# Feed-forward parts of 16, 16 and 12 feature tiles instead of 12, 16 and 16, and the spreading of 1/rms one step later

## The chip, the cores and the metric

The kernel runs on one core of a Trainium2 chip. The metric is the device time of one execution in microseconds (us); the time given for a kernel is the median of several executions. The profile shows the core's engines: TensorE (PE, with its weight loads as PEld), VectorE (DVE), ScalarE (ACT), GpSimd (POOL) and the DMA queue of SyncE (SP).

## What is computed

An encoder trunk of two residual layers on 256 tokens of width 2048, in float32. Layer 0 mixes tokens by grouped-query attention, layer 1 by a gated linear recurrence. Behind each mixer stands a feed-forward layer of 5632 features:

```python
def swiglu(h, w_gate, w_up, w_down):
    return (jax.nn.silu(h @ w_gate) * (h @ w_up)) @ w_down
...
        x = x + mix
        x = x + swiglu(rms_norm(x, norm_ffn[i]), ffn_w_gate[i], ffn_w_up[i], ffn_w_down[i])
```

## The kernel before

**Precision.** Every weight half (8 tiles of 128x128, 512 KB) is loaded into `raw`, rounded on ScalarE to `hi` (L142) and its remainder `lo` is made on VectorE (L144). Activations are split in the same way. A product of two operands is then three matmuls, hi·hi, hi·lo and lo·hi (`product`, L370 to L375).

**Tiling of the feed-forward layer.** The 5632 features are 44 tiles of 128, in three parts whose sizes are `PARTS` (L28). A part first makes its features, in units of four tiles (512 columns of gate and of up; 11 units in a layer, numbered through), then runs the part's rows of the down projection and adds them to the residual stream `x_tok`. The down projection handles its four columns of 512 in two pairs, c = 0 and c = 2 (`down`, L594).

**Two columns at a time, in seven products.** `project_pair` (L361) runs two columns, for units gate and up, over steps n of two row tiles each. A step that stands in `forms` is done in seven products rather than eight: `seven_forms` (L310) builds sums of weights on VectorE and ScalarE, and at the last such step of a pair `merge` (L415) combines the four extra sums. Which steps these are is set by `THREE` (1, 3, 5), for units listed in `FOURTH` also step `MORE` = 7, whose own operand form is built in the first such unit and kept, and with another order of the steps. For the down projection `down_seven` (L173) gives `THREE` for parts of 16 tiles (8 steps) and only its first two for parts of 12 (6 steps, `SHORT`). In `down_plan` (L166) the steps up to the last in seven products take both columns together; the others follow, first for the one column, then for the other, so that the first column is finished two halves before the second.

**The last part of layer 0.** There the second pair of columns is `alone`: it is done in plain products, first all steps of column 2, then all of column 3 (L189, L615). The reason is in the next stage: as each column is finished, `norm.add(c)` (L500) puts six pieces of work on the list `owed`: squares and transposes (`first`), four lots of copies (`copies`), and the scaled operands xg (`operands`). `settle` deals out one piece (two when more than six are owed) after each half; with the last column, all that is left is done at once. The recurrence's first projection, `project_two` (L441), uses the operands of columns 0 and 1 first, then those of column 2, and those of column 3 last.

**1/rms.** In that norm the factor 1/rms isn't in the operands. `spread` (L548) makes two diagonal matrices from it, and TensorE multiplies them by ones so that every partition has the row (L557); the result `nrb` scales the projections' outputs in `conv_branch` (L931). TensorE's program is in the order in which it is written; `later(NORM, stage)` places this product so many steps behind the call, where `step` is called once for each three matmuls of `sums`. `project_two` has 32 steps.

**Order on the engines.** TensorE's order is that of the program. The other engines' orders are made by a scheduler that simulates the program, within constraints: in the feed-forward layers the casts and remainders of the weights follow each other (`in_line`), copies stay behind the cast before them, and by `not_after` the remainder of the fourth half from there comes behind the adds that empty a finished column's accumulators (L609). `hi` and `lo` have five buffers each, `raw` six. Weight loads are issued by SyncE's queue, those prefetched for the sums of the steps in seven products by GpSimd's.

The lines that place the work:

```python
        return pair_plan(range(n), SHORT - 2 if n == SHORT else 1 + TWO[-1])
...
        return () if alone else THREE[:2] if n == SHORT else THREE
...
                alone = l == 0 and p == len(PARTS) - 1 and c > 0
...
                        settle(2 if len(owed) > 6 else 1)
...
            later(NORM, stage)
```

Of the kernel before, what the change touches and what calls it, by code (L numbers as in the profile page):

```python
# [24 lines left out]
GROUP = NQ // NKV  # L25
NBLK = 8
DFF = 5632
PARTS = [12, 16, 16]  # L28
THREE, TWO, SHORT = (1, 3, 5), (2, 5), 6
READY = 6  # L30
FOURTH, FOUR_STEPS, MORE = (3, 7), (1, 0, 3, 2, 5, 4, 7, 6), 7
FIRST_STEPS = (0, 1, 2, 4, 3, 6, 5, 7)
HALF = 8
WIDE = 512
# [6 lines left out]
GRID_W = 64  # L41

WARM = 10
NORM = 31
FIRST = 6
KEY_SCALE = 20
KEY_TURN = (62, 68)
# [24 lines left out]
def trunk(ctx, tc, w, out):  # L72
# [93 lines left out]
    def down_plan(n, alone):  # L166
        if alone:
            return pair_plan(range(n), 0)
        return pair_plan(range(n), SHORT - 2 if n == SHORT else 1 + TWO[-1])
# [6 lines left out]
    def ffn_order(l, base):  # L176
# [7 lines left out]

        for p, n in enumerate(PARTS):
            for _ in range(n // FOUR):
# [5 lines left out]
            for c in range(0, len(down), n):  # L192
                alone = l == 0 and p == len(PARTS) - 1 and c > 0
                for k, cols in down_plan(n // 2, alone):
# [54 lines left out]
    def later(delay, fn):  # L249
        waiting.append((clock[0] + delay, fn))  # L250
# [230 lines left out]
    class Norm:  # L481
# [66 lines left out]
        def spread(self):  # L548
# [11 lines left out]

            later(NORM, stage)

# [288 lines left out]
    def ffn(norm, nxt):  # L851
# [56 lines left out]
        line.update(act=None, dve=None)  # L908
        for p, n in enumerate(PARTS):
            hid, units, forms = [], [], {}  # L910
            for i in range(n // FOUR):
                unit(hid, units, forms, n, sum(PARTS[:p]) // FOUR + i)
            last = p == len(PARTS) - 1
            if last and nxt is not None:
# [237 lines left out]
```

## Time and profile before

| | |
|---|---|
| median of 3 executions | 1951.66 us (1951.56 to 1951.9) |
| the profiled execution | 1952.23 us |
| its span, first to last instruction | 1950.5 us |
| granted TensorE clock | 1.000 |
| read from HBM | 434.17 MB |

An engine's share on the page is its busy time over the span. In a row of a timeline stand start, length, engine, line, operation, the tile written, the tiles read, their shapes and how many instructions of the kind ran in a row; in brackets the idle time before it and what ended that. The last down projection of layer 0 runs from 860.65 to 945.65 us; the recurrent block begins there.

### The profile page before, as it was taken

The numbers are of one execution on the slowest core, as the hardware profiler recorded it, in microseconds if no ns is written. First come the engines' busy times: TensorE is split into PE (matmuls) and PEld (weight loads), VectorE is DVE, ScalarE is ACT, GpSimd is POOL, SyncE is SP. The second block draws the span as 40 slices with busy tenths as digits, with TensorE's granted clock in tenths as the row PEclk, the third lists the DMA queues.
The fourth block names the chain that finished last, engine by engine and source line by source line (L and its number), as shares of the span: only waits on it lengthen the run. The fifth ranks groups of instructions, "written<-read, shape, count | busy, mean of one in ns | idle before, by whom it ended". The sixth has DMA issues, their size and how long they took to land.

```text
span 1950.5 us, 27665 instructions
## 1 busy us (share of the span) xinstructions
PE 1944.6 (100%) x9623; PEld 1652.3 (85%) x9623; DVE 1751.0 (90%) x2362; ACT 1368.1 (70%) x2089; POOL 243.6 (12%) x345
## 2 busy tenths in 40 slices
PE   9999999999999999999999999999999999999999
PEld 7888888888888888888999998888888888888887
DVE  6777899999999999999878886999999999989997
ACT  6666777765777556777799886767756776567763
POOL 0011001011011110101034331011001010111010
PEclk9999999999999999999999999999999999999999
DMA  9544667778687787777555546577777777777784
GB/s 346 190 144 136 203 218 240 227 249 266 207 257 236 259 258 229 236 228 236 197 179 181 194 156 220 175 240 241 254 222 249 239 256 247 241 238 248 234 262 145
DMA packets 138091, 438.08 MB, mean 225 GB/s; under 512 B 15456, under 2 KB 16352, under 8 KB 137696
## 3 DMA queue, kind: packets, MB, share of 16 engines
q1 hardware_dynamic: 109296, 358.44, 53.3%
q0 software_dynamic: 28512, 77.87, 15.7%
q8 instruction: 75, 1.23, 0.2%
q14 instruction: 64, 0.52, 0.1%
q10 hardware_dynamic: 144, 0.02, 0.0%
HBM read 434.17 MB, written 2.10 MB: 224 GB/s over the span
## 4 chain that ended last, share of the span: by engine, by line
PE 98%; ACT 1%; DVE 0%; DMA 0%; issue 0%; SPq 0%; DVEq 0%; ACTq 0%
PE acc L372 61%; PE pm L372 14%; PE acc L274 10%; PE acc L425 3%; PE acc L426 3%; PE acc L427 3%; PE pm L274 1%; PE pm L427 1%; PE pm L426 1%; PE pm L425 1%; PE pm L763 1%; PE pm L795 1%; PE pm L781 0%; DMA raw<-in_w_qkv_dram 0%; ACT sg L627 0%; PE pm L707 0%
## 5 line engine op out<-in xcount | busy, mean ns | idle before, releaser
L144 DVE TENSOR_TENSOR lo<-raw,hi 128x1024 fp32r<-128x1024 f32 (+1 forms) x607 | 725.6, 1222 | 82.3 <-ACT hi L142 81.6
L142 ACT CAST hi<-raw 128x1024 fp32r<-128x1024 f32 (+1 forms) x607 | 618.2, 1045 | 213.8 <-PE acc L372 127.8
L372 PE MATMUL acc<-hi,xg 128*128 128x512 f32 x1836 | 588.3, 389 | 0.0
L372 PEld LDWEIGHTS acc<-hi,xg 128*128 128x128 f32 x1836 | 344.6, 188 | 71.8
L372 PE MATMUL acc<-hi,act 128*128 128x512 f32 x1258 | 401.9, 390 | 0.5 <-DVE gl L950 0.5
L372 PE MATMUL acc<-lo,xg 128*128 128x512 f32 x918 | 357.1, 389 | 0.0
L372 PEld LDWEIGHTS acc<-hi,act 128*128 128x128 f32 x1258 | 236.2, 188 | 49.8 <-DVE gl L950 0.9
L372 PE MATMUL acc<-lo,act 128*128 128x512 f32 x629 | 244.8, 389 | 0.0
L372 PEld LDWEIGHTS acc<-lo,xg 128*128 128x128 f32 x918 | 172.3, 188 | 35.6
L328 ACT CAST wxh<-raw 128x1024 fp32r<-128x1024 f32 x99 | 104.1, 1052 | 111.5 <-DVE raw L326 111.5
L323 ACT CAST hi<-sr 128x1024 fp32r<-128x1024 f32 x99 | 104.2, 1052 | 68.4 <-PE acc L372 60.7
L890 ACT COPY tf<-tb 32x256 f32<-32x256 f32 x352 | 142.1, 404 | 3.9
L425 PE MATMUL acc<-xg,hi 128*128 128x256 f32 x512 | 144.8, 283 | 0.0
L426 PE MATMUL acc<-xg,hi 128*128 128x256 f32 x512 | 144.6, 282 | 0.0
L427 PE MATMUL acc<-xg,lo 128*128 128x256 f32 x512 | 144.4, 282 | 0.0
L372 PEld LDWEIGHTS acc<-lo,act 128*128 128x128 f32 x629 | 118.1, 188 | 23.7
L324 ACT CAST wxh<-wx 128x512 fp32r<-128x512 f32 x99 | 61.4, 621 | 102.9 <-DVE wx L321 62.1
L330 DVE TENSOR_TENSOR wxl<-raw,wxh 128x1024 fp32r<-128x1024 f32 x99 | 120.4, 1216 | 3.6 <-ACT wxh L328 2.6
L327 DVE TENSOR_TENSOR lo<-sr,hi 128x1024 fp32r<-128x1024 f32 x99 | 120.5, 1217 | 0.0
L306 POOL DMA_DIRECT2D sr<-in_w_up_dram x70 | 39.1, 558 | 609.5 <-DVE lo L327 306.6
L274 PE MATMUL acc<-hi,xg 128*128 128x512 f32 x320 | 107.8, 397 | 0.0
L307 POOL DMA_DIRECT2D sr<-in_w_up_dram x70 | 60.6, 865 | 308.5 <-DMA sr<-in_w_up_dram 266.6
(216 smaller groups left out, 3438.9 us busy)
## 6 DMA issues: line engine op xcount, KB each, us to landing
raw<-in_w_gate_dram SPq DMA_DIRECT2D x176, 512.0 KB, 5.5
raw<-in_w_down_dram SPq DMA_DIRECT2D x147, 512.0 KB, 5.4
raw<-in_w_up_dram SPq DMA_DIRECT2D x106, 512.0 KB, 5.4
sr<-in_w_up_dram POOLq DMA_DIRECT2D x70, 512.0 KB, 4.7
raw<-in_w_in_dram SPq DMA_DIRECT2D x64, 512.0 KB, 4.4
raw<-in_w_qkv_dram SPq DMA_DIRECT2D x46, 512.0 KB, 4.6
wx<-in_w_up_dram SPq DMA_DIRECT2D x70, 256.0 KB, 3.6
sr<-in_w_up_dram POOLq DMA_DIRECT2D x70, 256.0 KB, 6.9
```

What stands on the lines that cost most here:

```text
L142: newest["cast"] = in_line("act", act.copy(hi[:, sl, :], raw[:, sl, :]))
L144: rest = in_line("dve", dve.tensor_tensor(lo[:, sl, :], raw[:, sl, :], hi[:, sl, :].bitcast(F32), ALU.subtract))
L274: pe.matmul(accs[a], x, wt[:, k, :], start=(k0 + k == 0 and n == 0), stop=(end and k == 1 and n == 2))
L323: in_line("act", act.copy(hi, raw))
L327: settled(in_line("dve", dve.tensor_tensor(lo, raw, hi[:].bitcast(F32), ALU.subtract)), taken[0] - 1)
L328: in_line("act", act.copy(xh[:, 1:, :], r1))
L330: in_line("dve", dve.tensor_tensor(xl[:, 1:, :], r1, xh[:, 1:, :].bitcast(F32), ALU.subtract))
L372: pe.matmul(acc, a, b, start=id(acc) not in begun, stop=last and i == 2)
L425: pe.matmul(o, hi, x[:, :S], start=start, stop=False)
L426: pe.matmul(o, hi, x[:, S:], start=False, stop=False)
L427: pe.matmul(o, lo, x[:, :S], start=False, stop=stop)
L890: n = act.copy(f[32 * i : 32 * i + 32, q::4, :, :], b[32 * q : 32 * q + 32, :, i, :, :])
```

## The change

The first two parts have 16 tiles, the last 12. The units that come first behind a down projection, and that use four steps in seven products, are now 4 and 8 instead of 3 and 7. The product of 1/rms with ones stands behind the 32nd step of the recurrence's first projection instead of the 31st, that is behind its last three matmuls.

```diff
-PARTS = [12, 16, 16]
+PARTS = [16, 16, 12]
...
-FOURTH, FOUR_STEPS, MORE = (3, 7), (1, 0, 3, 2, 5, 4, 7, 6), 7
+FOURTH, FOUR_STEPS, MORE = (4, 8), (1, 0, 3, 2, 5, 4, 7, 6), 7
...
-NORM = 31
+NORM = 32
```

The host slices the down weights by `PARTS` as well, so the arrays of layer parts change their sizes with it.

## The prediction

> **What bounds the kernel now.** I read the page's busy table and chain first, then TensorE's waits, then the longest pieces of the chain.
>
> ```profile
> span 1950.5 us, 27665 instructions
> ...
> PE 1944.6 (100%) x9623; PEld 1652.3 (85%) x9623; DVE 1751.0 (90%) x2362; ACT 1368.1 (70%) x2089; POOL 243.6 (12%) x345
> ...
> PE 98%; ACT 1%; DVE 0%; DMA 0%; issue 0%; SPq 0%; DVEq 0%; ACTq 0%
> ```
> ```profile
> PE pm L474 <- POOL ones L471: 1.0, 1, 1.0
> PE acc L274 <- DVE lo L144: 0.8, 1, 0.8
> PE acc L372 <- DVE gl L950: 0.5, 1, 0.5
> ```
> ```profile
> 890.73 55.08 PE acc L372 x243
> ```
>
> The reader should see that TensorE never stops. It is busy for 1944.6 of 1950.5 us, it is 98% of the chain, and the profile finds three waits in all, 2.3 us together: two at the start of the program and one at the last projection of the recurrent block. So time goes only where matmuls go, and any wait that the change brings is paid in full. The third fence prices a matmul: 243 of them, 512 columns wide, in 55.08 us without a break, 0.2267 us each. (Records overlap, so the mean of one, 389 ns, isn't the price.) A product is three of them, 0.68 us; half a weight group used the plain way is four products, 2.72 us.
>
> VectorE is the engine just behind, at 90%. How far it runs ahead shows in two rows:
>
> ```profile
> 513.54 1.22 DVE L327 TENSOR_TENSOR lo<-sr,hi 128x1024 fp32r<-128x1024 f32 x1
> ```
> ```profile
> 515.43 0.39 PE L372 MATMUL acc<-lo,nf 128*128 128x512 f32 x1
> ```
>
> The remainder `lo` of a weight half is finished at 514.76 and its first user starts at 515.43 (the matmul before this row still uses hi): 0.67 us of lead, the thinnest of the feed-forward layers. TensorE is the bound, VectorE is less than a microsecond from it at such places.
>
> **The change: matmuls.** A step in seven products replaces one in eight.
>
> ```profile
> L330 DVE TENSOR_TENSOR wxl<-raw,wxh 128x1024 fp32r<-128x1024 f32 x99 | 120.4, 1216 | 3.6 <-ACT wxh L328 2.6
> ```
>
> L330 runs once in each such step, so there are 99. Count them from the plans: each layer has 11 units with 3 and two of these with a fourth, 35, both before and after. A down projection of 16 tiles has 3 in each of its two column pairs, one of 12 has 2. Layer 1: 4+6+6 = 16 before, 6+6+4 = 16 after. In layer 0 the second pair of the last part has none: 4+6+3 = 13 before, 6+6+2 = 14 after. So 99 become 100: the columns that must do without lose two such steps, not three. **TensorE: minus 3 matmuls, 3 x 0.2267 = -0.68 us.** For VectorE, ScalarE and the DMA queues one more step of that kind adds some work where the first part now has 16 tiles; the next paragraph says why that is hidden.
>
> **The order of parts.** Before, a layer runs three units, a short down, four units, a down of 16, four units, a down of 16. After: four, 16, four, 16, three, short. Every neighbourhood of the new order exists already: units 0 to 3 in a row are like 4 to 6, units 4 and 8 with four steps follow a down of 16 as unit 7 does, a third unit goes into a short down as unit 2 does. None of these has a wait in the waits above. I cost them at nothing; the cover is the lead, and the thinnest is the 0.67 us quoted, in the unit behind unit 3. Unit 3 both builds an operand form and follows the short down; the new unit 4 builds it behind a down of 16. If this cover fails, a few tenths each time. What is new is only what comes behind the short down: in layer 1 the end of the program (same last columns, two plain steps each), in layer 0 the first norm of the recurrent block.
>
> **Layer 0's last down: where VectorE runs short.** While it finishes its columns, each finished column is squared, transposed, copied (L520) and turned into norm operands (L494, L495). These pieces are dealt out over the halves still to come. Before, from the end of the first column to the end of the down there are 2+16 = 18 halves; after, 2+12 = 14.
>
> ```profile
> 896.61:945.65 49.04, 49.04 (x219) 40.58 (x218) 44.50 (x71) 38.79 (x71) 7.25 (x4) 1.00 0.70 231
> ```
>
> The columns are window, PE, PEld, DVE, ACT and POOL busy. VectorE works 44.50 of 49.04 us. Without four halves the window is 49.04 - 4 x 2.72 = 38.16; the work falls by four remainders only, 4 x 1.15 (three in a row take 3.49, next fence): 39.9. To it comes what is left of the merge of the seven products. Compare the moment one column is done, in the short down and in the last:
>
> ```profile
> 403.16 3.49 DVE L144 TENSOR_TENSOR lo<-raw,hi 128x1024 fp32r<-128x1024 f32 x3
> ...
> 410.04 0.68 DVE L419 TENSOR_TENSOR fu<-pm,fg 128x512 f32<-128x512 f32 x1
> ...
> 411.23 0.68 DVE L420 TENSOR_TENSOR fg<-pm,fg 128x512 f32<-128x512 f32 x1
> 411.83 0.68 DVE L421 TENSOR_TENSOR fu<-fu,pm 128x512 f32<-128x512 f32 x1
> 412.43 0.68 DVE L601 TENSOR_TENSOR x_tok<-x_tok,fu 128x512 f32<-128x512 f32 x1
> ```
> ```profile
> 895.72 0.68 DVE L421 TENSOR_TENSOR fu<-fu,pm 128x512 f32<-128x512 f32 x1
> 896.31 0.68 DVE L601 TENSOR_TENSOR x_tok<-x_tok,fu 128x512 f32<-128x512 f32 x1
> ```
>
> In the short down VectorE is at L419 when the column ends (410.4), in the long one at the first of the last three L601 (896.6). Three operations of 0.6 more are owed: 39.9 + 1.8 = 41.7 us in 38.16. Not all of it is due. The remainders of the recurrence's second and third half (2 x 1.15) are used 2.9 us and more behind the down's end, and by the new count of steps the third column's operands (L495 x4, 1.7) come behind the last half: 41.7 - 2.3 - 1.7 = 37.7. Of this all but the recurrence's first remainder (1.15) must be done before the last half starts, 2.72 ahead of the end: 36.5 in 35.4. **A shortfall of about 1.1 us, which TensorE waits for.** Bounds: nothing, if the scheduler lets other pieces slide (the 4.5 us in which VectorE idled are not needed, the GpSimd loss below may go elsewhere); 1.1 + 1.35 if the idle time seen below recurs. I take 1.0, by the budget that rests on the nearest row. ScalarE: 38.79 - 4 x 1.0 = 34.8 of 38.16, not the bound.
>
> **The end of the norm and the product.** The fourth column's operands come last.
>
> ```profile
> 950.78 0.17 DVE L542 TENSOR_SCALAR nrt<-nrt 128x2 f32<-128x2 f32 x1
> 952.29 1.69 DVE L495 SCALAR_TENSOR_TENSOR xg<-tf,pk,xg 128x256 fp32r<-128x256 f32 x4 [1.35 <-ACT xg L494]
> ...
> 955.67 0.48 DVE L551 TENSOR_SCALAR ndg<-ident,nr 128x128 f32<-128x128 f32 x2
> ```
> ```profile
> 954.28 0.28 PE L425 MATMUL acc<-xg,hi 128*128 128x256 f32 x1
> ...
> 956.80 0.61 PE L557 MATMUL pm<-ndg,ones 128*128 128x128 f32 x4
> 957.16 0.36 PE L425 MATMUL acc<-xg,hi 128*128 128x256 f32 x1
> ```
>
> The recurrence starts at 945.65 and needs the fourth column's operands 72 matmuls of 0.12 us later, at 954.28; the first is ready at 952.7, 1.6 us early. After the change two remainders (2.3) stand before it, less 1.35 idle: 0.95 later, so 0.6 us remains and nothing is lost. The product L557 finds its operand ready at 956.15, 0.65 us before its turn. Later by 0.95 it would wait 0.3 us. One step later is three matmuls of 0.12, 0.36 us: it fits, at no cost on TensorE, with the same four matmuls. What it delays is the copy of 1/rms and the convolution behind it, by 0.36 us; their result is needed here:
>
> ```profile
> 962.31 0.76 DVE L455 TENSOR_TENSOR xs<-xc,xs 128x256 fp32r<-128x256 f32 x2
> ```
> ```profile
> 967.68 0.28 PE L425 MATMUL pm<-xs,ghi 128*128 128x256 f32 x1
> ```
>
> That is 4.6 us of slack. **Sum: -0.68 + 1.0 + 0 = +0.3 us.** The profiled execution took 1952.23 us, its span 1950.5 and 1.7 around it; the median of three is 1951.66, 0.57 lower. On the median the forecast is **1952.0 us**. No change: 0.2%, 3.9 us, is about what a measurement of this kernel can tell from no change.
>
> **Rivals.** (1) **No wait at all**: 1951.66 - 0.68 = 1951.0. For it speaks that the pieces are free to slide behind the remainders, against it that VectorE's work is more than the window.
>
> (2) **GpSimd in the way.** In this stretch GpSimd makes the remainders of four gate weights.
>
> ```profile
> L967 POOL TENSOR_TENSOR glo<-graw,ghi x32: 1292/1411/2345, 902.7 to 1150.5; 128x512 fp32r<-128x512 f32 x32
> ```
> ```profile
> 905.21 3.38 DVE L520 COPY tf<-tb 32x256 f32<-32x256 f32 x8
> ...
> 912.08 2.71 DVE L495 SCALAR_TENSOR_TENSOR xg<-tf,pk,xg 128x256 fp32r<-128x256 f32 x4
> ...
> 948.37 2.38 DVE L520 COPY tf<-tb 32x256 f32<-32x256 f32 x8
> ```
> ```profile
> 902.73 3.60 POOL L967 TENSOR_TENSOR glo<-graw,ghi 128x512 fp32r<-128x512 f32 x2 [32.88 <-ACT ghi L966]
> 909.67 3.65 POOL L967 TENSOR_TENSOR glo<-graw,ghi 128x512 fp32r<-128x512 f32 x2 [3.34 <-ACT ghi L966]
> ```
>
> Eight copies beside it take 3.38, alone 2.38; four operands 2.71 against the 1.69 above. So 2.0 us are lost by VectorE already, and are in the 44.50. Were VectorE held for the whole of each, 4 x 1.3 = 5.2, 3.2 more: 1952.0 + 3.2 = 1955.2. For it: no idle time is left in which to meet; against: GpSimd's pairs take 3.6 where twice the shortest is 2.6, so it waits as long itself.
>
> [...]
>
> (3) **Slower: remainders queued behind the adds.** A finished column's adds wait for TensorE, and VectorE runs in order. The kernel only asks that the remainder of the fourth half from there comes behind them; the scheduler may put the next half's there too. Then, at the end of the third column, TensorE waits for two adds, two transposes and the remainder: 2 x 0.6 + 2 x 0.65 + 1.2 = 3.7 us; with the shortfall 1952.0 + 3.7 = 1955.7. It decides as soon as the lead there is below one half. For it: the lead falls to about zero here; against: the half's cast stands before the pieces in the program.
>
> (4) **The fourth column's chain is late** by up to the 2.3 + 1.7 of work before it, less 1.35 idle and 1.6 early: 1.0 us, and the product as much again: 1953 to 1954.
>
> **Chances.** Forecast (a wait of 0.3 to 2 us, 1951.3 to 1953.0) 0.50; (1) 0.25; (2) 0.08; (3) 0.09; (4) 0.08. Range 1950.8 to 1954.6: it leaves out (3) and most of (2), some 0.15. Faster by over 0.2% (below 1947.8) has no mechanism, 2.3 us of waits and 0.68 of matmuls being all there is: 0.01. Slower by over 0.2% (above 1955.6) is (3): 0.09. Within: 0.90.
>
> **What would show it.** 9620 matmuls and 100 of L330. A wait "PE acc L372 <- DVE lo L144" near 925 to 945, of about 1 us, with VectorE busy without gaps ahead of it: the forecast; no such wait: (1); rows of L495 or L520 stretched beside L967: (2); one wait of 3 us right behind an L609: (3); L425 waiting for xg or L557 for ndg: (4). Wrong would be waits inside the units, or any part whose matmul period isn't 0.2267 us.

## The result and the profile after

| | before | after |
|---|---|---|
| median of 15 executions | 1951.9 us (1951.23 to 1952.76) | 1955.74 us (1954.29 to 1957.51) |
| the profiled execution | 1952.23 us | 1955.34 us |
| its span | 1950.5 us | 1953.5 us |
| mean granted clock | 1.000 | 0.999 |

The ratio is 1.0018, with a 95% interval of 1.0011 to 1.0025: slower by 3.8 us. That is outside the predicted range (1950.8 to 1954.6), 3.7 us above the forecast of 1952.0, which had expected almost no change.

The page of the changed kernel, span, busy times and the chain:

```profile
span 1953.5 us, 27662 instructions
...
PE 1945.5 (100%) x9620; PEld 1653.0 (85%) x9620; DVE 1756.0 (90%) x2367; ACT 1371.2 (70%) x2091; POOL 245.2 (13%) x347
...
PE 94%; DVE 2%; ACT 2%; DMA 1%; issue 1%; POOL 0%; SPq 0%; DVEq 0%; ACTq 0%; POOLq 0%
```

There are three matmuls fewer, as counted, and the chain of the end, 98% TensorE before, has other engines in it. TensorE's waits in the changed kernel (engine, tile and line that waited, what it waited for, total, times, longest):

```profile
PE acc L425 <- ACT xg L494: 2.1, 1, 2.1
PE pm L474 <- POOL ones L471: 1.0, 1, 1.0
PE acc L274 <- DVE lo L144: 0.6, 2, 0.4
PE acc L372 <- DVE gl L950: 0.2, 1, 0.2
PE acc L274 <- ACT hi L142: 0.2, 1, 0.2
```

One is new, and it is the first: the recurrence's first projection waits once, 2.1 us, for operands of the norm. No wait for a remainder stands in the down projection, where the forecast had put it. The place is found by the matmuls on either side, in TensorE's timeline: the recurrence's first, the one that waited, and the first product of gate weights.

```profile
944.69 0.28 PE L425 MATMUL acc<-xg,hi 128*128 128x256 f32 x1
...
955.61 0.38 PE L425 MATMUL acc<-xg,hi 128*128 128x256 f32 x1 [2.13 <-ACT xg L494]
...
971.04 0.28 PE L425 MATMUL pm<-xs,ghi 128*128 128x256 f32 x1
```

From the recurrence's start to the first gate product are 971.04 - 944.69 = 26.35 us; before they were 967.68 - 945.65 = 22.03. That is 4.3 us more for the same matmuls, of which the wait explains half. Most of the other half shows in the windows view and in two rows of the timeline behind the wait:

```profile
957.17 0.42 PE L426 MATMUL acc<-xg,hi 128*128 128x256 f32 x1
957.39 0.41 PE L427 MATMUL acc<-xg,lo 128*128 128x256 f32 x1
```
```profile
956.75:960.16 3.41, 3.41 (x17) 3.41 (x17) 3.26 (x9) 2.93 (x5) 0.20 (x4) 0.50 0.03 8
```

From 957.17 to 957.39 a matmul of 256 columns takes 0.21 us and not 0.12, and in the window the third number from the end is the granted clock: 0.50 for 3.41 us. The 4.3 us add up so: the matmul that waited starts 2.3 us later behind the recurrence's start than in the kernel before (955.61 - 944.69 against 954.28 - 945.65; 2.13 of it is the idle time in brackets); behind it come some 0.5 us of shorter stops while the operands arrive one by one; and 16 matmuls at half clock take 0.093 us more each, 1.5 us. The ledger of the two profiled executions, from rows of this kind: start to the feed-forward layer -0.3 (the program's start varies so much), layer 0's feed-forward 680.03 to 679.35, minus 0.68; the recurrence's start plus 4.3; the gates 202.24 in both; the way to layer 1's feed-forward -0.3; that layer 678.15 and 678.14; sum +3.0, as the spans have it.

**Why the operands are late.** VectorE at the end of the down projection, after:

```profile
942.85 2.36 DVE L144 TENSOR_TENSOR lo<-raw,hi 128x1024 fp32r<-128x1024 f32 x2
945.12 1.67 DVE L495 SCALAR_TENSOR_TENSOR xg<-tf,pk,xg 128x256 fp32r<-128x256 f32 x4
946.71 1.22 DVE L144 TENSOR_TENSOR lo<-raw,hi 128x1024 fp32r<-128x1024 f32 x1
947.84 0.68 DVE L609 TENSOR_TENSOR x_tok<-x_tok,acc 128x512 f32<-128x512 f32 x1
...
955.59 1.69 DVE L495 SCALAR_TENSOR_TENSOR xg<-tf,pk,xg 128x256 fp32r<-128x256 f32 x4 [1.34 <-ACT xg L494]
```

And the windows view, from the end of the first column to the down's end, and to the first add of the fourth column:

```profile
906.57:944.69 38.12, 38.12 (x170) 31.48 (x169) 37.64 (x63) 32.45 (x65) 7.69 (x4) 1.00 0.69 224
906.57:947.84 41.27, 41.27 (x196) 34.63 (x195) 40.79 (x68) 34.27 (x66) 7.69 (x4) 1.00 0.70 223
```

VectorE is busy 37.64 of 38.12 us and comes to the fourth column's add (L609) only at 947.84, 3.15 us behind the down's end. In the kernel before it did the first of the two adds at 944.49, 1.16 us ahead of the end:

```profile
944.49 0.69 DVE L609 TENSOR_TENSOR x_tok<-x_tok,acc 128x512 f32<-128x512 f32 x1 [1.77 <-PE acc L372]
```

Everything in the column's chain shifts with it: the operands start at 955.59, 10.9 behind the recurrence's start, where they did so 6.6 behind it.

### The profile page after: what moved, and what is told of

It is laid out like the page before. It is cut to its first block, busy times and chain, and to the rows that moved or that the text cites. A ratio compares the mean times of both kernels' runs of the same rounds, so it can differ in the third digit from the quotient of the medians.

```text
span 1953.5 us, 27662 instructions
## 1 busy us (share of the span) xinstructions
PE 1945.5 (100%) x9620; PEld 1653.0 (85%) x9620; DVE 1756.0 (90%) x2367; ACT 1371.2 (70%) x2091; POOL 245.2 (13%) x347
## 4 chain that ended last, share of the span: by engine, by line
PE 94%; DVE 2%; ACT 2%; DMA 1%; issue 1%; POOL 0%; SPq 0%; DVEq 0%; ACTq 0%; POOLq 0%
PE acc L372 58%; PE pm L372 14%; PE acc L274 10%; PE acc L426 3%; PE acc L425 3%; PE acc L427 3%; PE pm L274 1%; DVE lo L144 1%; PE pm L426 1%; PE pm L425 1%; PE pm L427 1%; PE pm L763 1%; PE pm L795 1%; DMA graw<-in_w_gates_dram 1%; PE pm L781 0%
## 5 line engine op out<-in xcount | busy, mean ns | idle before, releaser
L372 PE MATMUL acc<-hi,act 128*128 128x512 f32 x1244 | 397.9, 390 | 0.2 <-DVE gl L950 0.2
L425 PE MATMUL acc<-xg,hi 128*128 128x256 f32 x512 | 145.6, 284 | 2.1 <-ACT xg L494 2.1
L330 DVE TENSOR_TENSOR wxl<-raw,wxh 128x1024 fp32r<-128x1024 f32 x100 | 122.0, 1220 | 3.5 <-ACT wxh L328 2.3
L306 POOL DMA_DIRECT2D sr<-in_w_up_dram x70 | 38.9, 556 | 588.6 <-DVE lo L327 281.3
L425 PEld LDWEIGHTS acc<-xg,hi 128*128 128x128 f32 x512 | 98.7, 193 | 2.4 <-ACT xg L494 2.3
```

What stands on the lines that cost most here:

```text
L330: in_line("dve", dve.tensor_tensor(xl[:, 1:, :], r1, xh[:, 1:, :].bitcast(F32), ALU.subtract))
L372: pe.matmul(acc, a, b, start=id(acc) not in begun, stop=last and i == 2)
L425: pe.matmul(o, hi, x[:, :S], start=start, stop=False)
```

## Experiments

All times are medians; the kernel before ran on the same chip and is named beside each.

### Which layer

`PARTS` and `FOURTH` by layer, one layer changed; here for layer0_only, in layer1_only the two lists change places and `NORM` is 31:

```diff
-PARTS = [16, 16, 12]
+PARTS = [[16, 16, 12], [12, 16, 16]]
...
-                for k, cols in unit_plan(unit):
+                for k, cols in unit_plan(unit, l):
```

> Parts 16, 16, 12 in layer 0 alone, 12, 16, 16 in layer 1. Theory A (the loss is made at the end of layer 0's last down projection: TensorE waits 2.1 us for the fourth column's operands and then runs at half clock for 3.4 us): all of the change's time, about 1955.7 us, with the same wait of L425 for L494 and one stretch of clock 0.5. Rival B (the new order of units and downs costs in both layers): about half of the 3.8 us, 1953.8.

Measured 1955.61 us against 1951.88, ratio 1.0018 (1.0009 to 1.0027); the wait of L425 is 2.1 us again, and the clock is 0.86 over the 12 us from 950 on, which is one stretch of 0.50 for 3.41 us again.

> Parts 16, 16, 12 in layer 1 alone, layer 0 and the step of the product as before. It has 99 steps in seven products, as before. Theory A: the time of before, 1951.9 us within 0.4, no wait of L425, clock 1.0 up to the end. Rival B: about half of the 3.8 us, 1953.8.

Measured 1952.12 us against 1951.88, ratio 1.0001 (0.9992 to 1.001), no wait of L425. The whole loss is layer 0's: rival B falls.

### Which part of the order

```diff
-PARTS = [16, 16, 12]
+PARTS = [16, 12, 16]
...
+FOURTH, FOUR_STEPS, MORE = (4, 7), (1, 0, 3, 2, 5, 4, 7, 6), 7
```

> Parts 16, 12, 16 in both layers, units 4 and 7 with four steps, product behind the 32nd step. 99 steps in seven products. It has the changed kernel's first part and the last part of the kernel before. Theory A (only the short part at the end of layer 0 costs): 1951.9 us within 0.4, no wait of L425. Rival B2 (the longer first part has a share in the loss): 1952.6 or more.

Measured 1951.7 us against 1952.13, ratio 0.9997 (0.9988 to 1.0007). The profile's waits have nothing from the norm:

```profile
PE pm L474 <- POOL ones L471: 1.0, 1, 1.0
PE acc L372 <- DVE gl L950: 0.8, 1, 0.8
PE acc L274 <- DVE lo L144: 0.2, 1, 0.2
```

So the longer first part and the moved units cost nothing, as predicted. It is the short part at the end of layer 0.

### The product one step later, alone

```diff
-NORM = 31
+NORM = 32
```

> The kernel before with nothing but the product one step later. In its profile the operand was ready 0.65 us ahead of the product and the convolution 4.6 us ahead of its user. Theory A: no difference, 1951.9 within 0.4. Rival F (the later product, by the convolution behind it, has a part in the loss): 1952.5 us or more.

Measured 1951.81 us against 1952.09, ratio 0.9998 (0.9989 to 1.0007): without effect where its operand is early.

### Is the half clock a matter of standing still?

```diff
+FILLS = 8
...
+        spare = ps_m.tile([P, WIDE], F32, tag="pm", name=nm("pm"))
+        for i in range(FILLS):
+            for a in (0, 1):
+                pe.matmul(spare[:, a * S : a * S + S], rest[0][0][0], xs[0][:, :S], start=True, stop=True)
         for t, wt in zip(banks, rest):
             sums(t[:, :S], wt[n:], xs, HALF + n)
```

> The changed kernel with 16 extra matmuls of 256 columns, 16 x 0.12 = 1.9 us, into an accumulator that nobody reads, put just ahead of the twelve matmuls that wait for the fourth column's operands. The operands come no earlier, so TensorE can't go on earlier. Theory A1 (the half clock follows from TensorE standing still): the stretch of clock 0.5 goes and with it 1.6 us, about 1954.1, the wait shrinks to 0.2 us. Rival A2 (the clock falls for another reason, or the wait grows with the work ahead of it): 1955.7 or up to 1957.6, clock still 0.5 for 3.4 us.

Measured 1954.18 us against 1951.88, ratio 1.001 (1.0002 to 1.0019), 1.56 us below the changed kernel. The wait that is left, in the timeline (the inserted lines shift L494 to L499), and the window with its clock:

```profile
955.05 0.38 PE L426 MATMUL acc<-xg,hi 128*128 128x256 f32 x1 [0.25 <-ACT xg L499]
```
```profile
950.00:962.00 12.00, 11.56 (x92) 10.96 (x91) 10.17 (x26) 8.84 (x21) 0.20 (x4) 1.00 0.33 108
```

The operands come when they came: the matmul that needs them starts 10.96 us behind the recurrence's first, 10.92 in the changed kernel. TensorE does useless work meanwhile, and the kernel is faster, because the clock stays at 1.00; the mean clock is 1.000 in all eleven executions. A1 stands: of the loss, some 1.6 us are the clock's answer to a wait.

The other way round, the same wait was made in the kernel before, by idle additions between the fourth column's transposes and its copies, four of them in before_dose4 and six in before_dose6:

```diff
                 for a in range(2):
                     dve.transpose(fields["b"][:, a, :, :], x_tok[:, a, c, :])
+                if last and not self.seven:
+                    for i in range(4):
+                        junk = fields["f"][:, :4].rearrange("p q k t -> p (q k t)")
+                        dve.tensor_tensor(junk, x_tok[:, 0, c, :], x_tok[:, 1, c, :], ALU.add)
```

> The kernel before with four idle VectorE additions of 0.6 us between the fourth column's transposes and its copies: 2.4 us later, of which 1.6 were spare. Expected: L425 waits 0.8 us for the operands and L557 0.9 us for its matrix. Theory A1 (the half clock needs a wait of some length): if 0.8 and 0.9 are short enough, clock 1.0 and 1951.9 + 1.7 = 1953.6; if any wait of this kind brings it, 1953.6 + 1.6 = 1955.2.

Measured 1953.24 us against 1952.09, ratio 1.0003 (0.9994 to 1.0013). The wait is shorter than worked out, and the product's does not appear; the clock stays at 1.000:

```profile
954.96 0.39 PE L425 MATMUL acc<-xg,hi 128*128 128x256 f32 x1 [0.55 <-ACT xg L494]
```

> The same with six additions, 3.6 us: L425 waits 2.0 us, as in the changed kernel, L557 0.9. Theory A1: the clock falls to 0.5 for 3.4 us as it does there, 1951.9 + 2.9 + 1.6 = 1956.4. Rival A2 (the half clock has to do with something else in the changed kernel): clock 1.0, 1954.8.

Measured 1955.44 us against 1952.09, ratio 1.0016 (1.0007 to 1.0026). Its waits, and a window around its half clock:

```profile
PE acc L425 <- ACT xg L494: 2.0, 1, 2.0
```
```profile
950.00:962.00 12.00, 9.88 (x69) 9.46 (x68) 10.31 (x26) 8.13 (x16) 0.20 (x4) 0.86 0.14 44
```

0.86 over 12 us is one stretch of 0.5 for 3.4. So 1.2 us more of VectorE work, from four additions to six, cost 2.2 us: the clock again, but not in every execution. The mean clock is 0.999 in five of the ten, whose median is 1957.18 us, and 1.000 in the other five, with a median of 1954.67; 3.41 us at 0.50 take the mean of such a span to 0.999. Rival A2 falls all the same, since nothing here is the changed kernel's but the wait. The forecast of 1956.4 had the product's wait of 0.9 in it, which does not appear in the trace; that the slow matmuls ahead of it hid it is likely, not shown.

### Is it VectorE's load? GpSimd out of the way

```diff
         act.copy(hi, raw)
+        if n < GATE_BUFS:
+            follow(i, newest["operand"][0])
```

(`i` is the copy; the last operand of the norm on ScalarE.)

> The changed kernel with the casts of the first four gate weights ordered behind the last of the fourth column's operands on ScalarE, so that GpSimd's four remainders (L967) can't meet VectorE in the last down projection. VectorE lost 2 to 4 us to them there. Theory C (VectorE's backlog at the end of the down projection is what makes the fourth column late, and GpSimd's share of it is enough to matter): the wait of L425 falls from 2.1 us to under 0.5, the clock stays at 1.0, 1951.2 to 1951.9 us. Rival D (the pieces are late by the order in which they are dealt, not by VectorE's load): the wait stays near 2 us, 1955 us or more.

Measured 1953.11 us against 1951.88, ratio 1.0006 (0.9997 to 1.0015). VectorE now comes to the fourth column's add at 944.96, 0.5 us behind the down's end (944.48) and not 3.15, and L425 waits no longer for the norm:

```profile
944.96 0.69 DVE L609 TENSOR_TENSOR x_tok<-x_tok,acc 128x512 f32<-128x512 f32 x1
```

What waits instead:

```profile
956.24 0.44 PE L557 MATMUL pm<-ndg,ones 128*128 128x128 f32 x2
957.42 0.49 PE L557 MATMUL pm<-ndg,ones 128*128 128x128 f32 x2 [0.74 <-DVE ndg L551]
958.56 0.38 PE L427 MATMUL acc<-xg,lo 128*128 128x256 f32 x1 [0.41 <-DVE lo L144]
```
```profile
954.91 2.45 DVE L551 TENSOR_SCALAR ndg<-ident,nr 128x128 f32<-128x128 f32 x2
```

The two matrices that the product takes in took 2.45 us, 0.48 before, while GpSimd's first two remainders ran (954.72 to 957.28). Theory C is right about the backlog, and rival D, in which the load has no part, falls, but GpSimd's cost moved on, and the time of 1951.2 to 1951.9 was missed.

In gates_later the four casts were ordered behind the copy of 1/rms, which follows the product; the last change below is in gates_later4 alone:

```diff
-                act.copy(self.r, pst[:, :S])
+                newest["nrb"] = act.copy(self.r, pst[:, :S])
...
+            follow(i, newest["nrb"])
...
-        raw = tmp("graw", (P, 4, P), bufs=2)
+        raw = tmp("graw", (P, 4, P), bufs=4)
```

> As gates_late, but the four casts stand behind the copy of 1/rms on ScalarE (L559), so that GpSimd's remainders begin only when the product has been made. In gates_late the two diagonal matrices (L551) took 2.45 us beside GpSimd where 0.48 is usual, and TensorE waited 0.7 us for the product and 0.4 for a remainder. Theory C: with these gone too, no wait at the end of the norm and the gain of one step in seven products is left: 1951.2 us (1950.9 to 1951.6), clock 1.0. Rival E (the four gate weights come too late for the first gate product, or block the convolution, so that the wait only moves on): a wait at L425 for ghi, glo or xs, 1952.5 us or more.

Measured 1954.31 us against 1952.09, ratio 1.0011 (1.0002 to 1.0019), from 1952.14 to 1956.66; 1951.2 was missed. The execution whose trace is kept was the fastest, and has no wait there; what the others waited for isn't in a trace.

> As gates_later, but with four raw buffers for the gate weights, not two, so that their loads don't wait for each other's casts. In gates_later the third weight landed only at 964.5 us in the one execution profiled, its remainder ended as late as 971, and the times of eleven executions lay between 1952.1 and 1956.7. Theory C: with the loads early, the wait at the end of the norm is gone in all executions, 1951.2 us (1950.9 to 1951.8), spread as before. Rival E (GpSimd's remainders in the convolution's stretch make TensorE wait there instead): above 1952.5, with waits of L425 for xs, ghi or glo.

Measured 1952.42 us against 1952.13, ratio 1.0001 (0.9992 to 1.001), from 1951.96 to 1952.86: the loads were what made the times spread. It takes back 3.3 of the 3.8 us, but is no faster than the kernel before. The profile shows where more than the 0.68 went: a wait for a remainder that VectorE made late beside GpSimd (of two like casts ahead of it, the one at 962.75, while GpSimd's four remainders ran from 958.32 to 963.95, took 1.48 us, the one at 964.48 took 0.28), and shorter stops at the operands and at the product.

```profile
PE acc L427 <- DVE lo L144: 0.4, 1, 0.4
```

Its recurrence takes 23.3 us to the first gate product, not 22.0; 0.7 of the 1.3 us are at this wait. Theory C's 1951.2 was missed by 1.2.

### Order against load

```diff
-                    dve.transpose(fields["b"][:, a, :, :], x_tok[:, a, c, :])
+                    turned = dve.transpose(fields["b"][:, a, :, :], x_tok[:, a, c, :])
+                if last and not self.seven:
+                    not_after(turned, 2)
```

> The changed kernel with the remainders of the recurrence's third and fourth half ordered behind the fourth column's two transposes on VectorE. VectorE's work stays the same; two pieces that aren't due yet (2 x 1.15 us) no longer stand ahead of the transposes. Theory G (what delays the fourth column is the order: work that isn't due stands ahead of it): the second transpose ends 2.3 us earlier against the down's end; the copies on VectorE then come behind the two remainders, so the first L494 is earlier by 1.0 only, L425 waits about 1.1 us; three more remainders now stand ahead of L551, so L557 waits, 1.5 us or so. 1953.5 to 1955.5 by whether the clock falls. Rival D2 (order is without effect, the whole is VectorE's load): L425 waits 2.1 us as before.

Measured 1958.8 us against 1952.13, ratio 1.0035 (1.0021 to 1.0049), with four executions from 1957.91 to 1961.36 and one of 6429.18; the forecast was 1953.5 to 1955.5. Its waits:

```profile
PE pm L559 <- DVE ndg L553: 2.9, 1, 2.9
PE acc L425 <- ACT xg L494: 1.3, 1, 1.3
```

The wait for the operands fell from 2.1 to 1.3 with the same work (1.1 was expected), so the order does count; the remainders put off stood ahead of the product's matrices instead, and that wait came out at 2.9 rather than 1.5, with a half clock of 6.8 us (mean clock 0.998). VectorE has little room there, two stops of 0.43 and 0.54 us from 946.32 to the matrices at 960.65, so the work put off delayed what it was put in front of.

## Why the prediction was wrong

**Right**: the matmuls (9620, and 100 of L330; -0.68 us, to the hundredth in layer 0's feed-forward layer); the order of parts, which costs nothing (layer1_only, middle12); the product one step later, free (norm32_only); the layer, the stretch and the engine that runs short. Rival (4) had the shape of what happened and was given 0.08, at 1953 to 1954.

**The step that failed** is the reading of VectorE's budget: "Not all of it is due." The sum itself held. 41.7 us were forecast up to where the window of before ends, 1.16 us behind its first fourth-column add, so 40.5 up to that add; 40.79 were measured. From them I took off 4.0 us that TensorE didn't need yet, let TensorE pay 1.1 us of the remainder in the down projection, and left the fourth column's chain with 0.95 of delay. The trace of after shows those 4.0 us ahead of the fourth column's add: of the three remainders from 942.85 to 947.84, the second and third, and the four L495 are the very rows I had called deferrable. In VectorE's order what isn't due still stands in front of what is. No remainder came late in the down projection, so TensorE paid nothing there, and all of it fell on the chain behind: 10.9 - 6.6 = 4.3 us later, not 0.95, against 2.0 us to spare at the first operand's rounded part (in the row below the first of four is ready at 952.3; it is used at 954.28). That leaves 2.3, and 2.13 were waited.

```profile
951.77 1.70 ACT L494 ACTIVATE xg<-tf,pk 128x256 fp32r<-128x256 f32 x4
```

The 0.95 had a misread row in it as well: the 1.35 us of idle time ahead of L495, which were to absorb a part of the delay, are a wait for ScalarE within the same chain, behind the adds. They shift with it, and the row of after still has 1.34. So of the forecast's sum the term +1.0, the wait in the down projection, measured 0, and the term 0, the end of the norm, measured +4.3, the stops and the half clock behind the wait included.

Two runs show both sides of it: with the order changed (turn_first) the wait falls by 0.8, with GpSimd's share of the load gone it vanishes (gates_late).

**The term that was missing** is the clock. A wait was priced at its length. The changed kernel's 2.1 us bring another 1.6, shown from both directions by fill (the same wait, filled, without the half clock, 1.56 us faster) and before_dose6 (the same wait made elsewhere, with it). Together 2.3 + 0.5 + 1.5 - 0.68 = 3.6, beside the 3.8 measured.

**The rivals.** (1), no wait, is the gain that none of the versions here got. (2), GpSimd: not 3.2 us more, but its share in the backlog was decisive, 2.7 us of VectorE's time by gates_late (3.15 - 0.5), of which the 44.50 of the prediction already held 2.0. (3), remainders queued behind the adds, did not happen.

## What to carry to other kernels

When a fixed amount of side work is dealt out over fewer steps, compare the side engine's whole work up to the critical piece with the time up to it; work that nobody needs yet counts in full if it stands ahead in that engine's order. A wait of TensorE of 2.1 us cost 4.3 here in the traced execution, with the stops and the half clock behind it; so a gain of three matmuls isn't worth a risk of one such wait. A second engine's work that is moved out of one contended stretch must have a stretch to go to: in gates_late the two matrices took 2.45 us beside the remainders that were moved, and 0.48 before.

## What was not expected of the hardware

The granted clock fell to 0.50 for 3.41 us shortly behind a single wait of 2.0 to 2.1 us (in the changed kernel from 956.75 to 960.16; in layer0_only and before_dose6 by the 0.86 over 12 us), for 6.8 us with two waits of 1.3 and 2.9 (turn_first, mean clock 0.998), and not behind waits of 0.55, or 0.74 and 0.41 (before_dose4, gates_late, mean clock 1.000).

Here are the 3.41 us ahead of the fall in the changed kernel, then two stretches of that length in turn_first, the second of them just ahead of its fall (the second number is TensorE's busy time):

```profile
953.34:956.75 3.41, 1.14 (x7) 0.81 (x6) 2.01 (x7) 3.35 (x10) 0.00 (x0) 1.00 0.19 72
```
```profile
953.19:956.60 3.41, 2.01 (x13) 1.82 (x14) 2.44 (x7) 2.71 (x7) 0.20 (x4) 1.00 0.42 155
956.60:960.02 3.42, 1.51 (x13) 1.30 (x11) 3.36 (x3) 2.03 (x4) 0.00 (x0) 1.00 0.31 96
```

TensorE stood still for 2.27 us just ahead of the fall in the changed kernel and for 1.91 in turn_first; behind the stretch with 1.40 the clock was still 1.00. What else decides it is not shown. The changed kernel's mean clock is 0.999 in twelve of 15 executions and 1.000 in three, the two fastest among them, and layer0_only has eight of eleven and before_dose6 five of ten at 0.999; no trace of an execution with such a wait and a mean of 1.000 is kept, so why these are at 1.000 is not shown.
